# Hybrid stream step: the scan's decays behind the index heads, modulation blocks 4, 5 and 11 elsewhere

## The chip, the cores and the metric

The kernel runs on one core of a Trainium2 chip. The core has a matrix engine (TensorE, "PE" in the profile, its weight loads "PEld"), a vector engine (VectorE, "DVE"), a scalar engine (ScalarE, "ACT"), a general engine (GpSimd, "POOL") and a queue that starts transfers (SyncE, "SP"). They run side by side, and each works through its own list of instructions in the order written down. The metric is the device time of one execution in microseconds (us); lower is better.

## The reference, cut to what matters

One layer of a streaming encoder with d_model 1024 is computed for 512 new frames and 64 frames that follow a cache of 512; together 576 rows. A conditioning vector c gives six modulation vectors of 1024 numbers each:

```python
mod = (silu(c) @ w_ada + b_ada)            # 6 * 1024 columns
sh1, sc1, gt1, sh2, sc2, gt2 = split(mod, 6)
h = rms_normalize(x) * g_norm_mix * (1 + sc1) + sh1
q, k, v, qi, ki, wi, z, xbc, dt, gate = split(h @ w_in)
```

Branch A is sparse attention. Small index heads, `qi` (8 heads of 64) and `ki`, are turned by a rotation (rope) and give each query a score for every key; the 128 or 144 best keys of each query are kept, and attention runs over these. Branch B is a state-space scan: `dt` gives step sizes, and from them decays, `acs = cumsum(softplus(dt + dt_bias) * -exp(a_log))` within chunks, weigh the scan. Both branches are projected, gated and summed; `x = x + gt1 * mixed`. A gated feed-forward net follows, on `rms_normalize(x) * g_norm_ffn * (1 + sc2) + sh2`, and its result is added after a product with `gt2`.

## The kernel before, in words

**Number format.** Weights arrive as float32 (`raw`, two buffers) and are split into a high part `wh` (a copy on ScalarE) and a low part `wl` (raw minus high, on VectorE), three buffers each. Each product is three matmuls: high by high, high by low, low by high. Activations are split likewise (`hTh`, `hTl`).

**Stages.** Start: load, normalise, compute sh1 and sc1, make h. Then the first products with `w_in`: a small one (`misc`: ki, wi, dt), two gate columns, the index heads `qi0` and `qi1` (function `tm`, 256 columns each), then k, v, the first two groups of q, and gate columns as filler work for TensorE. While TensorE does these, VectorE computes scores and takes the best keys by repeated maxima (the index stage, until about 235 us). Attention follows per key head, with more filler columns; then the scan (about 470 to 800 us), the branch projections (to about 930), the output projection, the feed-forward net, and at the end the down projection `w_down` in eight columns of 128 with the residual (`x2r`) and the transposes back.

**Modulation blocks.** `w_ada` is worked on in blocks of 512 columns, u = 0 to 11. Blocks for sh1 and sc1 are made in the start. Blocks 4 and 5 are gt1, 6 and 7 sh2, 8 and 9 sc2, 10 and 11 gt2. `ada_columns(u, pool)` (line 765) makes one: four transfers of 512 KB (`adr`, two buffers), 16 VectorE instructions that accumulate (`aacc`), eight small matmuls that pick the sums (with a reserve, below), a copy `ra`, a transpose and an addition into `modc`. Before, blocks 4 and 5 are called behind the index stage's code (line 1174, pool `adx`), 6 to 9 in the branch projections (line 1528, pool `adv`), 10 and 11 ahead of the down projection (line 1816).

**Decays.** Behind `misc` stand the decays (from `dcol` to `acs_d`): softplus on tiles `dtp` and `e1` to `e3` ("e" in the profile) as a chain of small VectorE instructions, `dA`, then 15 small matmuls with the triangles `tri` and `ones` into PSUM, and their read-out into `nacs`, `edec`, `wst`, `acsT`.

**Index heads.** `key_stack` (line 1087) doubles the keys on GpSimd (`kisd`), transposes them on TensorE and splits them into `kis`. `rope` (line 966) rotates `x` (tile `tok`): two VectorE products into `tmpb`, one GpSimd product in place, one VectorE addition. `q_stack` (line 1106) transposes the heads and splits them into `qis`. Scores start from `kis` and `qis`.

**What sets the order.** The program isn't issued as written. `Plan` (from line 246) collects all instructions with their data dependences, gives each a cost (`cost`) and lays them out with a list scheduler (`order`, line 391): it takes the engine that is free first and gives it, of its ready instructions, the one of lowest rank; the rank is the place in the program minus an offset (`with R.prio(4000)` moves work ahead; weight splits after the first have it). An engine with something ready is never left idle on purpose. `R.slack` is a reserve: a TensorE instruction counts as ready only so many us after its inputs (0.25 by default, 3.0 for the pick matmuls). `with R.after(ops)` makes instructions count as ready only behind `ops`, in the plan alone. The order found is then fixed for each engine; on the chip an instruction waits for its true inputs. Buffers of a tag are handed out in program order: `px` has two PSUM slots and `py` two, so an instruction that gets a slot waits for all readers of the tile that had it before. A pool opens only when the pools closed ahead of it in the program are done (`R.close`): attention's pool behind `ix` and `adx`, the feed-forward net's behind `adv`.

Of the kernel before, what the change touches and what calls it, by code (L numbers as in the profile page):

```python
# [13 lines left out]
P = 128  # L14
# [225 lines left out]


NADA = 0
NADX = 2
NRAW, NWH = 2, 3
SLACK = 0.25

# [294 lines left out]
def build(tc, I, O):  # L541
# [13 lines left out]
    def px(name, tag="px"):  # L555
        return psum.tile([P, 512], F32, name=name, tag=tag, bufs=2)
# [409 lines left out]
    def rope(name, x, tab, h, rms):  # L966

        x4 = x.rearrange("p t (h d) -> p t h d", h=h)
        b = ap_.tile([P, 5, h, HD], F32, name=name + "rb", tag="tmpb", bufs=1)
        if rms:  # L970
            act.activation(b, x4, AF.Square)
            r = ap_.tile([P, 5, h], F32, name=name + "rr", tag="rr", bufs=2)
            vec.tensor_reduce(r, b, axis=AX.X, op=OP.add)
            rf = r.rearrange("p t h -> p (t h)")
            rstd_of(rf, rf, 5 * h, P, HD)
            vec.tensor_tensor(x4, x4, r[:, :, :, None].to_broadcast([P, 5, h, HD]), OP.mult)
        vec.tensor_tensor(b[..., 0:32], x4[..., 32:64], tab[:, :, None, 64:96].to_broadcast([P, 5, h, 32]), OP.mult)
# [56 lines left out]
    sync.dma_start(O["ki_sample"][0, 0], ki[:NS, 4, :])  # L1034


    dcol = cp.tile([P, 16], F32, name="dcol")
    for r in range(2):
        pool.tensor_copy(dcol[64 * r:64 * r + 64], dsk[64 * r:64 * r + 64].rearrange("p (b r) -> p r b", r=2)[:, r])
    act.activation(alg, alg, AF.Exp)  # L1040
    dtp = cp.tile([P, 5, 32], F32, name="dtp")
    e1 = ix.tile([P, 5, 32], F32, name="e1")
    e2 = ix.tile([P, 5, 32], F32, name="e2")
    e3 = ix.tile([P, 5, 32], F32, name="e3")
    vec.tensor_tensor(dtp, misc[:, :, 72:104], dtb[:, None, :].to_broadcast([P, 5, 32]), OP.add)
    act.activation(e1, dtp, AF.Abs)
    act.activation(e1, e1, AF.Exp, scale=-1.0)
    vec.tensor_scalar(e2, e1, 2.0, None, op0=OP.add)
    vec.reciprocal(e2, e2)
    vec.tensor_tensor(e1, e1, e2, OP.mult)  # L1050
    vec.tensor_tensor(e2, e1, e1, OP.mult)
    vec.tensor_scalar(e3, e2, 1.0 / 17.0, None, op0=OP.mult)
    for c in (15.0, 13.0, 11.0, 9.0, 7.0, 5.0, 3.0):
        vec.scalar_tensor_tensor(e3, e3, 1.0 / c, e2, op0=OP.add, op1=OP.mult)
    vec.scalar_tensor_tensor(e3, e3, 1.0, e1, op0=OP.add, op1=OP.mult)
    vec.tensor_scalar(dtp, dtp, 0.0, None, op0=OP.max)
    vec.scalar_tensor_tensor(dtp, e3, 2.0, dtp, op0=OP.mult, op1=OP.add)
    dA = e1
    vec.scalar_tensor_tensor(dA, dtp, -1.0, alg[:, None, :].to_broadcast([P, 5, 32]), op0=OP.mult, op1=OP.mult)
    pool.memset(dA[NS:P, 4, :], 0.0)  # L1060
    nacs = cp.tile([P, 5, 32], F32, name="nacs")
    wst = cp.tile([P, 5, 32], F32, name="wst")
    edec = cp.tile([P, 5, 32], F32, name="edec")
    p = px("pacs")
    p2 = px("ptot", "py")
    for c in range(5):
        pe.matmul(p[:, 32 * c:32 * c + 32], tri, dA[:, c, :], start=True, stop=True)
        pe.matmul(p2[:, 32 * c:32 * c + 32], ones, dA[:, c, :], start=True, stop=True)
    fl = lambda z: z.rearrange("p c h -> p (c h)")
    vec.tensor_scalar(fl(nacs), p[:, :160], -1.0, None, op0=OP.mult)  # L1070
    act.activation(fl(edec), p2[:, :160], AF.Exp)
    vec.tensor_tensor(fl(wst), p2[:, :160], fl(nacs), OP.add)
    act.activation(wst, wst, AF.Exp)
    vec.tensor_tensor(wst, wst, dtp, OP.mult)
    p = [px("pacsTa"), px("pacsTb", "py")]
    for c in range(5):
        o, i0 = (p[0][:32, P * c:P * c + P], P) if c < 4 else (p[1][:32, :NS], NS)
        pe.matmul(o, dA[:i0, c, :], tri[:i0, :i0], start=True, stop=True)
    acsT = ix.tile([32, T], F32, name="acsT")
    act.activation(acsT[:, :NP_], p[0][:32, :], AF.Copy)  # L1080
    act.activation(acsT[:, NP_:], p[1][:32, :NS], AF.Copy)
    acs_d = R.dram([32, T], F32, name="acs_d")
    sync.dma_start(acs_d, acsT)
# [22 lines left out]
    def q_stack(st, name, x, pair, h0, n_h):  # L1106


        p = px(f"{name}p")
        p2 = px(f"{name}q", "py")  # L1110
        for tb in range(4):
            pe.transpose(p[:, tb * P:(tb + 1) * P], x[:, tb, P * pair:P * pair + P], ident)
        pe.transpose(p2[:, 0:P], x[:, 4, P * pair:P * pair + P], ident)
        for i in range(2):
            for src, c0, n in ((p, (h0 + i) * NP_, NP_), (p2, n_h * NP_ + (h0 + i) * NS, NS)):
                d = st[:, c0:c0 + n]
                act.activation(d[0:64], src[64 * i:64 * i + 64, :n], AF.Copy)
                vec.tensor_tensor(d[64:128], src[64 * i:64 * i + 64, :n], d[0:64].bitcast(F32), OP.subtract)

    kis = key_stack(ix, "kis", "kis", ki, I["cache_ki"][0, 0].rearrange("(t p) d -> p t d", p=P))  # L1120
    qis = ix.tile([P, 8 * T], F32R, name="qis")
    for hf in range(2):
        x = ap_.tile([P, 5, 256], F32, name=f"qi{hf}", tag="tok", bufs=2)
        tm(f"qi{hf}", getw(), 256, x)
        rope(f"qi{hf}", x, cs2, 4, False)
        for pr in range(2):
            q_stack(qis, f"qis{hf}{pr}", x, pr, 4 * hf + 2 * pr, 8)


    masks = []  # L1130
# [5 lines left out]
    for b in (4, 1, 2, 3):  # L1136
        smp = b == 4
        n = T if smp else P * (b + 1)
        rows = NS if smp else P
        k0 = NP_ if smp else 0  # L1140
        s = ix.tile([P, n], F32, name=f"score{b}")
        for h in range(NIH // 2 if smp else NIH):
            q0 = 8 * NP_ + h * P if smp else h * NP_ + b * P
            q = qis[:, q0:q0 + P]
            w1 = wi2[:, h:h + 1] if smp else wi[:, b, h:h + 1]
            for c0, cn in (((0, TH), (TH, TH)) if smp else ((0, n),)):
                ps = px(f"pix{b}_{h}_{c0}", "py")
# [19 lines left out]
        vec.tensor_scalar(masks[b][:rows], s[:rows, :n], -2.0e38, NEG, op0=OP.is_gt, op1=OP.mult)  # L1167
# [714 lines left out]
```

## Time and profile before

| | us |
|---|---|
| median of 3 runs | 1392.15 |
| lowest and highest run | 1389.15, 1392.44 |
| the profiled execution | 1395.28 |
| its span, first to last instruction | 1393.5 |
| PE busy in the span | 1363.9 |

The profile comes from one execution. Helper calls issue all instructions, so every row has line 533, and rows are told apart by their tiles: `out<-in`, buffer numbers left out (`wh3` is `wh`, `e1` is `e`, `hTh` stays). A timeline row has start, duration, engine, instruction, tiles, shape, count; in brackets stands how long the engine was idle before it and what ended that. Neighbouring instructions of one kind are merged into a row with their count. A table by stage has for each stretch the busy time of each engine with its instruction count, the granted clock of PE as a share, the share of the DMA engines that was busy, and GB/s; for one tile it counts that tile's instructions alone. A float32 matmul that isn't split has two entries in the trace.

### The profile page before, as it was taken

The numbers are of one execution on the slowest core, as the hardware profiler recorded it, in microseconds if no ns is written. First come the engines' busy times: TensorE is split into PE (matmuls) and PEld (weight loads), VectorE is DVE, ScalarE is ACT, GpSimd is POOL, SyncE is SP. The second block draws the span as 40 slices with busy tenths as digits, with TensorE's granted clock in tenths as the row PEclk, the third lists the DMA queues.
The fourth block names the chain that finished last, engine by engine and source line by source line (L and its number), as shares of the span: only waits on it lengthen the run. The fifth ranks groups of instructions, "written<-read, shape, count | busy, mean of one in ns | idle before, by whom it ended". The sixth has DMA issues, their size and how long they took to land.

```text
span 1393.5 us, 27697 instructions
## 1 busy us (share of the span) xinstructions
PE 1363.9 (98%) x10801; PEld 1323.5 (95%) x10801; DVE 1052.8 (76%) x2099; ACT 721.8 (52%) x1496; POOL 243.2 (17%) x366
## 2 busy tenths in 40 slices
PE   7989999999999999999999999999999999999998
PEld 5989999999999999999999999999999999999998
DVE  4488999687877798989887688834899888875221
ACT  5435233667876667666665342225666666661221
POOL 1210001530310254655554200000000000000000
PEclk9999999999999999999999999999999999999999
DMA  9943345764754454544435598646233333346331
GB/s 283 281 140 92 87 119 151 171 153 122 166 134 126 136 143 123 145 125 143 130 110 172 177 311 262 206 136 189 72 92 102 96 91 92 90 130 202 107 109 29
DMA packets 268836, 200.17 MB, mean 144 GB/s; under 512 B 24993, under 2 KB 240193, under 8 KB 268705
## 3 DMA queue, kind: packets, MB, share of 16 engines
q1 hardware_dynamic: 265680, 187.39, 45.8%
q0 software_dynamic: 3024, 11.01, 4.3%
q8 instruction: 85, 1.39, 0.4%
q14 instruction: 47, 0.38, 0.1%
HBM read 157.81 MB, written 29.55 MB: 134 GB/s over the span
## 4 chain that ended last, share of the span: by engine, by line
PE 81%; DVE 7%; DMA 4%; issue 3%; ACT 2%; POOL 1%; SPq 1%; ACTq 0%; POOLq 0%; DVEq 0%
PE mm L533 59%; PE py L533 14%; PE px L533 9%; DVE score L533 1%; DMA raw<-in_w_in 1%; DVE aacc L533 1%; DVE wl L533 1%; DVE m L533 1%; SPq L533 1%; DMA stage<-y_d 1%; DMA adr<-in_w_ada 1%; DMA xt<-in_x_sample 1%; DMA wl<-raw 1%; ACT wh L533 0%; DMA bc<-acs_d 0%
## 5 line engine op out<-in xcount | busy, mean ns | idle before, releaser
L533 ACT ACTIVATE wh<-raw 128x1024 fp32r<-128x1024 f32 (+2 forms) x159 | 156.3, 985 | 245.4 <-PE mm L533 178.1
L533 PE MATMUL mm<-hTh,wl 128*128 128x288 f32 (+1 forms) x1024 | 235.8, 303 | 0.0
L533 PE MATMUL mm<-hTh,wh 128*128 128x288 f32 (+1 forms) x1024 | 235.0, 305 | 0.4 <-ACT hTh L533 0.4
L533 PE MATMUL mm<-hTl,wh 128*128 128x288 f32 (+1 forms) x1024 | 232.8, 303 | 0.0
L533 DVE TENSOR_TENSOR wl<-raw,wh 128x1024 fp32r<-128x1024 f32 (+2 forms) x116 | 139.9, 1208 | 84.4 <-ACT wh L533 81.4
L533 PEld LDWEIGHTS mm<-hTh,wh 128*128 128x128 f32 (+1 forms) x1024 | 167.4, 189 | 3.7 <-issue 1.3
L533 PEld LDWEIGHTS mm<-hTh,wl 128*128 128x128 f32 (+1 forms) x1024 | 167.8, 189 | 2.7 <-issue 1.4
L533 PEld LDWEIGHTS mm<-hTl,wh 128*128 128x128 f32 (+1 forms) x1024 | 166.8, 189 | 2.7 <-issue 1.4
L533 DVE SCALAR_TENSOR_TENSOR cu<-xc,wc,cu 128x579 f32<-128x579 f32 x96 | 84.7, 883 | 2.6 <-ACT cu L533 2.0
L533 PE MATMUL mm<-fh,wl 128*128 128x288 f32 x352 | 80.2, 299 | 0.9 <-DVE x2r L533 0.9
L533 PE MATMUL mm<-fh,wh 128*128 128x288 f32 x352 | 80.4, 298 | 0.1
L533 PE MATMUL mm<-fl,wh 128*128 128x288 f32 x352 | 80.5, 298 | 0.0
L533 PE MATMUL mm<-wl,hTh 128*128 128x256 f32 x256 | 73.6, 288 | 5.0 <-DVE wl L533 4.5
L533 PE MATMUL mm<-wh,hTl 128*128 128x256 f32 x256 | 73.0, 287 | 0.0
L533 PE MATMUL mm<-wh,hTh 128*128 128x256 f32 x256 | 72.6, 287 | 0.0
L533 DVE SCALAR_TENSOR_TENSOR aacc<-adr,sil,aacc 128x512 f32<-128x512 f32 x98 | 69.4, 746 | 0.9 <-DMA adr<-in_w_ada 0.7
L533 PEld LDWEIGHTS mm<-fh,wl 128*128 128x128 f32 x352 | 58.0, 189 | 1.9 <-DVE x2r L533 1.4
L533 PEld LDWEIGHTS mm<-fh,wh 128*128 128x128 f32 x352 | 58.1, 189 | 0.6 <-ACT wh L533 0.3
L533 PEld LDWEIGHTS mm<-fl,wh 128*128 128x128 f32 x352 | 58.1, 189 | 0.3 <-issue 0.2
L533 PE MATMUL mm<-yl,wh 128*128 128x288 f32 x256 | 54.9, 297 | 1.1 <-DVE yl L533 1.0
L533 PE MATMUL mm<-yh,wl 128*128 128x288 f32 x256 | 55.9, 297 | 0.0
L533 PE MATMUL mm<-yh,wh 128*128 128x288 f32 x256 | 55.1, 298 | 0.1
(439 smaller groups left out, 3768.4 us busy)
## 6 DMA issues: line engine op xcount, KB each, us to landing
raw<-in_w_in SPq DMA_DIRECT2D x80, 512.0 KB, 4.1
adr<-in_w_ada SPq DMA_DIRECT2D x48, 512.0 KB, 6.2
rawu<-in_w_gate_up SPq DMA_DIRECT2D x22, 512.0 KB, 3.9
raw<-in_w_gate_up SPq DMA_DIRECT2D x22, 512.0 KB, 3.8
wl<-raw POOLq DMA_DIRECT2D x21, 512.0 KB, 4.9
bc<-acs_d SPq DMA_DIRECT2D x32, 256.0 KB, 3.6
raw<-in_w_branch_ssm SPq DMA_DIRECT2D x16, 512.0 KB, 4.1
raw<-in_w_down SPq DMA_DIRECT2D x16, 512.0 KB, 3.6
```

Source lines behind the costliest of these rows:

```text
L533: getattr(engines[x.eng], x.fn)(*[real(a) for a in x.args], **{k: real(v) for k, v in x.kw.items()})
```

## The change

`NADX` goes from 2 to 1. The text of `key_stack`, `q_stack` and the loop over the two index heads moves as it is from behind the decays to ahead of them; `rope` now returns its last instruction, and the loop keeps it. The decays' 15 matmuls get a reserve of 3 us. The block loop behind the index takes block 4 alone and ties it to the first head's rotation; block 5 falls to the loop of `adv`, which now runs over 5 to 9 (its code is the same and depends on `NADX`). Block 11 moves from ahead of the loop over the eight columns of the down projection to ahead of the second of them. A list `masked` is filled and not used.

```diff
-NADX = 2
+NADX = 1
...
-        vec.tensor_tensor(x4, x4, b, OP.add)
+        return vec.tensor_tensor(x4, x4, b, OP.add)
...
+    kis = key_stack(ix, "kis", "kis", ki, I["cache_ki"][0, 0].rearrange("(t p) d -> p t d", p=P))
+    qis = ix.tile([P, 8 * T], F32R, name="qis")
+    ropes, masked = [], []
+    for hf in range(2):
+        x = ap_.tile([P, 5, 256], F32, name=f"qi{hf}", tag="tok", bufs=2)
+        tm(f"qi{hf}", getw(), 256, x)
+        ropes.append(rope(f"qi{hf}", x, cs2, 4, False))
+        for pr in range(2):
+            q_stack(qis, f"qis{hf}{pr}", x, pr, 4 * hf + 2 * pr, 8)
     dcol = cp.tile([P, 16], F32, name="dcol")
...
+    R.slack = 3.0
     p = px("pacs")
     p2 = px("ptot", "py")
...
         pe.matmul(o, dA[:i0, c, :], tri[:i0, :i0], start=True, stop=True)
+    R.slack = SLACK
     acsT = ix.tile([32, T], F32, name="acsT")
...
-    for hf in range(2):
-        x = ap_.tile([P, 5, 256], F32, name=f"qi{hf}", tag="tok", bufs=2)
-        tm(f"qi{hf}", getw(), 256, x)
-        rope(f"qi{hf}", x, cs2, 4, False)
-        for pr in range(2):
-            q_stack(qis, f"qis{hf}{pr}", x, pr, 4 * hf + 2 * pr, 8)
...
-    with R.prio(0):
-        for u in range(4, 4 + NADX):
+    for u, op in ((4, ropes[0]),):
+        with R.after([op]):
             ada_columns(u, adx)
...
-    ada_columns(11, adg, 1, 4)
-    vec.tensor_scalar(gt2h[:, 4:8], gt2[:, 4:8], 0.5, None, op0=OP.mult)
     yop = R.mkpool("yout", reuse_waits="tile")
     fd = (lambda k: fh[k], lambda k: fl_[k])
     for a in range(8):
+        if a == 1:
+            ada_columns(11, adg, 1, 4)
+            vec.tensor_scalar(gt2h[:, 4:8], gt2[:, 4:8], 0.5, None, op0=OP.mult)
         w = getw()
```

More of the change, by code (lines that the diff above doesn't have):

```diff
@@ L1034, in build @@
     sync.dma_start(O["ki_sample"][0, 0], ki[:NS, 4, :])
[L1037 to L1083, printed above, removed]
     def key_stack(pl, tag, name, new, cache, kd=None):
@@ L1124, in build @@
         tm(f"qi{hf}", getw(), 256, x)
-        rope(f"qi{hf}", x, cs2, 4, False)
+        ropes.append(rope(f"qi{hf}", x, cs2, 4, False))
         for pr in range(2):
             q_stack(qis, f"qis{hf}{pr}", x, pr, 4 * hf + 2 * pr, 8)
+    dcol = cp.tile([P, 16], F32, name="dcol")
+    for r in range(2):
+        pool.tensor_copy(dcol[64 * r:64 * r + 64], dsk[64 * r:64 * r + 64].rearrange("p (b r) -> p r b", r=2)[:, r])
+    act.activation(alg, alg, AF.Exp)
+    dtp = cp.tile([P, 5, 32], F32, name="dtp")
@@ new lines, in build @@
+    e1 = ix.tile([P, 5, 32], F32, name="e1")
+    e2 = ix.tile([P, 5, 32], F32, name="e2")
+    e3 = ix.tile([P, 5, 32], F32, name="e3")
+    vec.tensor_tensor(dtp, misc[:, :, 72:104], dtb[:, None, :].to_broadcast([P, 5, 32]), OP.add)
+    act.activation(e1, dtp, AF.Abs)
+    act.activation(e1, e1, AF.Exp, scale=-1.0)
+    vec.tensor_scalar(e2, e1, 2.0, None, op0=OP.add)
+    vec.reciprocal(e2, e2)
+    vec.tensor_tensor(e1, e1, e2, OP.mult)
+    vec.tensor_tensor(e2, e1, e1, OP.mult)
+    vec.tensor_scalar(e3, e2, 1.0 / 17.0, None, op0=OP.mult)
@@ new lines, in build @@
+    for c in (15.0, 13.0, 11.0, 9.0, 7.0, 5.0, 3.0):
+        vec.scalar_tensor_tensor(e3, e3, 1.0 / c, e2, op0=OP.add, op1=OP.mult)
+    vec.scalar_tensor_tensor(e3, e3, 1.0, e1, op0=OP.add, op1=OP.mult)
+    vec.tensor_scalar(dtp, dtp, 0.0, None, op0=OP.max)
+    vec.scalar_tensor_tensor(dtp, e3, 2.0, dtp, op0=OP.mult, op1=OP.add)
+    dA = e1
+    vec.scalar_tensor_tensor(dA, dtp, -1.0, alg[:, None, :].to_broadcast([P, 5, 32]), op0=OP.mult, op1=OP.mult)
+    pool.memset(dA[NS:P, 4, :], 0.0)
@@ new lines, in build @@
+    nacs = cp.tile([P, 5, 32], F32, name="nacs")
+    wst = cp.tile([P, 5, 32], F32, name="wst")
+    edec = cp.tile([P, 5, 32], F32, name="edec")
+    R.slack = 3.0
+    p = px("pacs")
+    p2 = px("ptot", "py")
+    for c in range(5):
+        pe.matmul(p[:, 32 * c:32 * c + 32], tri, dA[:, c, :], start=True, stop=True)
+        pe.matmul(p2[:, 32 * c:32 * c + 32], ones, dA[:, c, :], start=True, stop=True)
+    fl = lambda z: z.rearrange("p c h -> p (c h)")
+    vec.tensor_scalar(fl(nacs), p[:, :160], -1.0, None, op0=OP.mult)
@@ new lines, in build @@
+    act.activation(fl(edec), p2[:, :160], AF.Exp)
+    vec.tensor_tensor(fl(wst), p2[:, :160], fl(nacs), OP.add)
+    act.activation(wst, wst, AF.Exp)
+    vec.tensor_tensor(wst, wst, dtp, OP.mult)
+    p = [px("pacsTa"), px("pacsTb", "py")]
+    for c in range(5):
+        o, i0 = (p[0][:32, P * c:P * c + P], P) if c < 4 else (p[1][:32, :NS], NS)
+        pe.matmul(o, dA[:i0, c, :], tri[:i0, :i0], start=True, stop=True)
+    R.slack = SLACK
+    acsT = ix.tile([32, T], F32, name="acsT")
+    act.activation(acsT[:, :NP_], p[0][:32, :], AF.Copy)
@@ L1130, in build @@
+    act.activation(acsT[:, NP_:], p[1][:32, :NS], AF.Copy)
+    acs_d = R.dram([32, T], F32, name="acs_d")
+    sync.dma_start(acs_d, acsT)
     masks = []
@@ L1166, in build @@
             vec.match_replace(s[:rows, :n], m8[:rows], s[:rows, :n], -3.0e38)
-        vec.tensor_scalar(masks[b][:rows], s[:rows, :n], -2.0e38, NEG, op0=OP.is_gt, op1=OP.mult)
+        masked.append(vec.tensor_scalar(masks[b][:rows], s[:rows, :n], -2.0e38, NEG, op0=OP.is_gt, op1=OP.mult))
         if smp:
```

## The prediction

> **What bounds the kernel now.** I read the page first, then the table by stage, then the PE gaps one by one, then the queue of the engine that ended each gap.
>
> ```profile
> PE 1363.9 (98%) x10801; PEld 1323.5 (95%) x10801; DVE 1052.8 (76%) x2099; ACT 721.8 (52%) x1496; POOL 243.2 (17%) x366
> ```
>
> TensorE is busy for 1363.9 of 1393.5 us. The change removes no PE instruction, so it can only win back idle PE time, 29.6 us in all, and time in which PE ran slowly. The table by stage says where the edited region loses (columns: stretch, us, busy of PE, PEld, DVE, ACT, POOL with counts, granted clock, DMA share, GB/s).
>
> ```profile
> 60.00:80.00 20.00, 15.85 (x126) 15.66 (x125) 13.60 (x27) 5.11 (x8) 5.07 (x8) 0.90 0.82 248
> 80.00:100.00 20.00, 20.00 (x162) 19.67 (x162) 14.96 (x28) 7.58 (x18) 3.93 (x2) 0.93 0.40 114
> 260.00:280.00 20.00, 17.92 (x147) 17.48 (x146) 14.55 (x31) 13.77 (x28) 11.02 (x6) 1.00 0.56 124
> ```
>
> From 60 to 80 us PE is idle for 4.15 us, and the granted clock is 0.90 and 0.93 there instead of 1.00. PE's timeline shows one gap and a slow stretch behind it:
>
> ```profile
> 73.14 0.28 PE L533 MATMUL mm<-wh,hTh 128*128 128x256 f32 x1
> 73.26 0.27 PE L533 MATMUL mm<-wl,hTh 128*128 128x256 f32 x1
> 77.68 0.58 PE L533 MATMUL mm<-wl,hTh 128*128 128x256 f32 x1 [4.15 <-DVE wl L533]
> ...
> 78.91 0.42 PE L533 MATMUL mm<-wh,hTh 128*128 128x256 f32 x1
> 79.12 0.42 PE L533 MATMUL mm<-wl,hTh 128*128 128x256 f32 x1
> ...
> 82.54 0.35 PE L533 MATMUL mm<-wl,hTh 128*128 128x256 f32 x1
> ```
>
> PE ran dry at 73.53 in the second product of the index heads (qi1) and waited until 77.68 for the low half `wl` of a weight split. Before the gap a matmul started every 0.12 us, behind it every 0.21 us, until 82.54. Next, VectorE's queue ahead of that `wl`, the same engine's share for block 4 alone (tile aacc), and ScalarE's part:
>
> ```profile
> 68.46 0.48 DVE L533 TENSOR_SCALAR aacc<-adr,sil 128x512 f32<-128x512 f32 x1 [0.58 <-DMA adr<-in_w_ada]
> ...
> 74.79 0.74 DVE L533 SCALAR_TENSOR_TENSOR aacc<-adr,sil,aacc 128x512 f32<-128x512 f32 x1
> 75.46 1.03 DVE L533 SCALAR_TENSOR_TENSOR e<-e,e 128x160 f32<-128x160 f32 x3
> 76.41 1.22 DVE L533 TENSOR_TENSOR wl<-raw,wh 128x1024 fp32r<-128x1024 f32 x1
> ```
> ```profile
> 68.00:76.40 8.40, 0.00 (x0) 0.00 (x0) 5.33 (x8) 0.97 0.71 195
> ```
> ```profile
> 70.38 2.03 ACT L533 ACTIVATE wh<-raw 128x1024 fp32r<-128x1024 f32 x2 [0.23 <-PE mm L533]
> ```
>
> `wh`, which `wl` needs, was done at 70.38 + 2.03/2 = 71.40. `wl` began at 76.41 only because eight instructions of modulation block 4 and the decay chain (tile e) stood ahead of it. VectorE works in the order written down, so the stall is one of order.
>
> **The change, part by part.** *Block 4 behind the first rotation.* Its eight instructions leave this queue. An instruction starts about 0.07 us before its predecessor's end (74.79 + 0.74 = 75.53, the next at 75.46), so they hold 5.33 - 8 x 0.07 = 4.77 us. `wl` would start at 76.41 - 4.77 = 71.64, be done at 72.86, and PE needs it at 73.53: the 4.15 us go, with 0.67 us to spare. What may be put in this place instead is the rest of the decay chain, and the key stack of the index, which could not run so early before:
>
> ```profile
> 76.40:95.00 18.60, 3.53 (x30) 3.25 (x30) 1.66 (x6) 0.00 (x0) 0.12 (x1) 0.83 0.42 117
> ```
> ```profile
> 94.42 1.29 DVE L533 TENSOR_TENSOR kis<-px,kis 128x512 fp32r<-128x512 f32 x2 [0.25 <-ACT kis L533]
> ```
>
> These are 1.66 us (six instructions of the chain) and 1.29 us. With both ahead, `wl` is done at 72.86 + 2.95 = 75.81 and 2.28 us of stall stay. Gain between 1.87 and 4.15; I take 4.15, because the computed case stands on the queue as it is.
>
> *The clock.* 77.68 to 82.54 is 4.86 us at a pitch of 0.213, some 23 matmuls. At 0.12 they take 2.74, so 2.1 us are lost to the low clock. A gap of 4.15 us was followed by it. The stretch 260 to 280, which has 2.08 us idle, kept 1.00. So without the gap the 2.1 us come back, and with 2.28 us left it is open. I take 2.1, with 0 as the other end. The Trainium skill, "TensorE: Matmul & The Clock Gate", section "Why this matters for your kernels", warns of PE gaps over about 3 us; by that rule a rest of 2.28 us would keep the full clock too, and both rows here agree with it.
>
> *Index heads ahead of the decays.* The two PSUM slots of tag px are given out in program order. Before, the index's transposes took theirs behind the decays' sums:
>
> ```profile
> 67.07 0.72 POOL L533 COPY kisd<-misc 128x640 f32<-128x640 f32 x1 [2.72 <-issue]
> 85.14 1.49 DVE L533 TENSOR_TENSOR tok<-tok,tmpb 128x1280 f32<-128x1280 f32 x1 [2.85 <-POOL tok L533]
> ```
> ```profile
> 91.23 1.06 PE L533 MATMUL px<-tri,e 128*32 128x128 f32 x8
> ...
> 92.79 0.60 PE L533 MATMUL px<-ident,kisd 128*128 128x128 f32 x4
> ...
> 96.14 0.60 PE L533 MATMUL px<-ident,tok 128*128 128x128 f32 x4
> ```
>
> The keys were ready at 67.79 and turned at 92.79; the first heads were rotated at 86.63 and turned at 96.14. In the new order they need no decay. That moves some 10 to 20 us of latency, which PE filled with matmuls, so it is worth nothing by itself. It does make the order tighter: the first heads' transposes now stand right behind their rotation, as the second heads' did, and those waited. All waits of PE from 85 to 300 us:
>
> ```profile
> PE px L533 <- DVE P L533: 1.6, 1, 1.6
> PE px L533 <- DVE tok L533: 0.7, 1, 0.7
> PE py L533 <- ACT lg L533: 0.6, 1, 0.6
> PE mm L533 <- DMA wl<-raw: 0.5, 1, 0.5
> PE mm L533 <- DVE wl L533: 0.3, 1, 0.3
> PE py L533 <- DVE qis L533: 0.3, 1, 0.3
> ```
>
> I charge one more wait of the tok kind: 0.7 us lost. Its ends are 0 and 0.7 + 0.9, since the two rotations on POOL differed by 0.87 us:
>
> ```profile
> 81.30 3.81 POOL L533 TENSOR_TENSOR tok<-tok,cs 128x1280 f32<-128x1280 f32 x1 [13.51 <-DVE tmpb L533]
> 104.37 2.94 POOL L533 TENSOR_TENSOR tok<-tok,cs 128x1280 f32<-128x1280 f32 x1 [17.26 <-DVE tmpb L533]
> ```
>
> The Trainium skill, "SBUF — State Buffer", section "Who interferes with whom", says that a VectorE instruction with two SBUF inputs contends with a GpSimd instruction that reads SBUF. By it, decays and splits beside both rotations would make both take 3.81 and the sum would be 0.9 us less; the longer rotation here did have VectorE instructions beside it.
>
> *The reserve of 3 us* moves the 15 small decay matmuls later in PE's order; they are the same in number. If VectorE were later still than the reserve, the weight matmuls queued behind them on PE would wait. No row of before has PE waiting there, so nothing is charged. The whole stretch is ordered anew, though. For that the six rows above are the nearest price, 4.0 us in all: as much may go or come. I take zero and keep both ends.
>
> *Block 5 to the branch stage.* It leaves the index stage and joins blocks 6 to 9 behind 811 us, with four loads of 512 KB on SP, 16 VectorE instructions, eight small matmuls (16 entries in the trace), a transpose and two small VectorE copies:
>
> ```profile
> 118.00:240.00 122.00, 0.85 (x16) 0.32 (x16) 11.31 (x16) 1.00 0.40 113
> ```
> ```profile
> 906.00:933.00 27.00, 27.00 (x205) 27.00 (x204) 10.30 (x16) 6.58 (x10) 0.96 (x8) 1.00 0.33 101
> ```
> ```profile
> 885.74 0.28 DVE L533 COPY ra<-px 128x128 f32<-128x128 f32 x1
> 904.91 0.28 DVE L533 COPY ra<-px 128x128 f32<-128x128 f32 x1
> ```
> ```profile
> 834.04 4.74 SPq L533 DMA_DIRECT2D adr<-in_w_ada  x2
> ...
> 933.62 2.00 SPq L533 DMA_DIRECT2D x<-x_d  x4
> ```
>
> Two blocks end 19.2 us apart, so a fifth ends at 904.9 + 19.2 = 924.1, ahead of the next stage's loads at 933.62. VectorE is free for 16.7 of the 27 us from 906 and needs 11.3. Cover is there; cost zero on both sides, as PE does the same work in either place. If SP's queue loses that cover, the price is in the slower rival.
>
> *Block 11 behind the first column of the last stage.* Before, its instructions stood ahead of the residual x2r, for which PE's transposes waited:
>
> ```profile
> 1267.51 4.72 DVE L533 SCALAR_TENSOR_TENSOR aacc<-adr,sil,aacc 128x512 f32<-128x512 f32 x7
> ...
> 1273.95 0.79 DVE L533 SCALAR_TENSOR_TENSOR x2r<-mm,gt2h,x2r 128x32 f32<-128x32 f32 x3
> ```
> ```profile
> 1274.25 0.28 PE L533 MATMUL px<-ident,x2r 128*32 128x128 f32 x1 [0.88 <-DVE x2r L533]
> ```
>
> Gain 0.9 us, with 0 as the other end. Its results are needed only from the fifth column on.
>
> **The sum:** 4.15 + 2.1 + 0.9 - 0.7 = 6.45 us. The profiled execution took 1395.28 us (span 1393.5 and 1.78 around it) and would take 1388.8. The median of the runs shown is 1392.15, 3.13 lower; against it 1385.7.
>
> **The rivals.** *VectorE's queue stays full* (22%): the chain and the key stack take block 4's place. For it: the planner never leaves an engine idle that has something ready, and the decays are ready early. Against it: the 0.67 us of room and the rank of `wl`. Gain 1.87 + 0 + 0.9 - 0.7 = 2.1 us, 1390.1. *The index stage gains as well* (14%): with 11.31 us less on VectorE the 4.0 us of waits go and none is added: 6.45 + 0.7 + 4.0 = 11.2, 1381.0. For it: the stage's splits and rotations share VectorE with that block. Against it: the largest of the waits, 1.6 us for P, lies in the attention, behind the index. *SP held by block 5's loads* (9%), the one that ends slower: a load of modulation weights waits on SP until VectorE has read the buffer, 4.74 us in the row at 834, and the weights queue behind it. A weight tile feeds 48 matmuls, 27/205 x 48 = 6.3 us; holds beyond that lead stop PE. Four loads held so long are 19.0 us, 12.7 beyond the lead: 12.7 - 6.45 = 6.2 us slower, 1398.4. Against it: PE is busy for all 27 us of the row from 906, right behind four such blocks. *The change doesn't do what it says* (5%): the planner places the decays where they were and only the last stage gains 0.9, 1391.3.
>
> **How the numbers follow.** The forecast has 50%, and its own range is 1383 to 1388. A measurement of this kernel can tell about 0.3% (4.2 us) from no change. Faster by more: 50 + 14 = 64%. Within it: 22 + 5 = 27%. Slower: 9%. The range goes from the second rival's 1381.0 less half the spread of the runs shown (1.6) to no change with 1.6 more: 1379.5 to 1394.0; outside lie the slower rival and little else.
>
> **What would show it.** Right: no PE gap in the qi1 product, granted clock 1.00 from 60 us on, transposes of kisd ahead of the matmuls with tri, no aacc instruction until the first rotation has ended, no PE wait for x2r at the start of the last stage. Wrong: a PE wait for `wl` of over 2 us between 60 and 100, waits for tok of over 1 us, SP holds ahead of the branch weights with PE idle behind 811, or x loads later than PE's need.

## The result, and the profile after

The changed kernel took 1384.67 us (median of 6 runs, 1383.1 to 1386.53), the kernel before 1390.7 us beside it (median of 6, 1389.15 to 1392.44). The ratio is 0.9956, 95% interval 0.9943 to 0.9969: 6.1 us faster. The profiled execution took 1384.84 us (span 1383.1). That of before took 1395.28, which is 4.6 above the median of its runs here, so the 10.4 us between the two profiles overstate the gain.

The page of the changed kernel, its line of engines:

```profile
PE 1357.8 (98%) x10801; PEld 1319.1 (95%) x10801; DVE 1053.1 (76%) x2099; ACT 721.3 (52%) x1496; POOL 246.4 (18%) x366
```

Same counts, and PE is busy for 6.1 us less: it ran less of its work slowly. Idle PE time fell from 29.6 to 25.3 us. Where, in the table by stage (60 to 80 and 80 to 100 answer to the two rows of before):

```profile
60.00:80.00 20.00, 18.99 (x160) 18.81 (x161) 13.20 (x27) 6.41 (x11) 4.14 (x7) 1.00 0.53 163
80.00:100.00 20.00, 19.44 (x165) 19.23 (x164) 12.92 (x20) 6.84 (x14) 5.95 (x2) 1.00 0.45 139
```

From 60 to 80 PE did 160 matmuls instead of 126, at a granted clock of 1.00 instead of 0.90 and 0.93. The gap in the qi1 product and the slow stretch behind it are gone. But PE's waits from 60 to 120 (us in total, times, longest) are not:

```profile
PE px L533 <- DMA kisd<-in_cache_ki: 2.3, 1, 2.3
PE py L533 <- DVE wst L533: 1.0, 1, 1.0
PE px L533 <- DVE kis L533: 0.9, 1, 0.9
PE mm L533 <- DVE wl L533: 0.6, 1, 0.6
```

They are 4.7 us where before had 5.1 (4.1 for `wl`, 0.7 and 0.3). PE's timeline of the changed kernel shows the first and the third in their places, and VectorE's what became of `wl`:

```profile
60.09 0.63 PE L533 MATMUL px<-ident,kisd 128*128 128x128 f32 x4 [2.26 <-DMA kisd<-in_cache_ki]
...
70.12 0.33 PE L533 MATMUL px<-ident,kisd 128*128 128x128 f32 x1 [0.92 <-DVE kis L533]
...
75.62 0.40 PE L533 MATMUL mm<-wh,hTh 128*128 128x256 f32 x2
```
```profile
72.50 0.33 DVE L533 SCALAR_TENSOR_TENSOR e<-dtp,alg 128x160 f32<-128x160 f32 x1
74.42 2.36 DVE L533 TENSOR_TENSOR wl<-raw,wh 128x1024 fp32r<-128x1024 f32 x2 [1.60 <-ACT wh L533]
81.98 1.49 DVE L533 TENSOR_TENSOR tok<-tok,tmpb 128x1280 f32<-128x1280 f32 x1 [3.15 <-POOL tok L533]
89.02 0.88 DVE L533 TENSOR_SCALAR aacc<-adr,sil 128x512 f32<-128x512 f32 x2
```

The transposes of the cached keys now stand in PE's order ahead of the index heads' products, and their transfer had not landed: PE stood for 2.26 us, then 0.92 for the split of the first transposes. The decay chain ended at 72.83, ahead of `wl`, and `wl` began at 74.42, not at the forecast 71.64; it waited for `wh`, with nothing else to do. `wh` in turn had waited on ScalarE for PE:

```profile
73.33 2.01 ACT L533 ACTIVATE wh<-raw 128x1024 fp32r<-128x1024 f32 x2 [0.23 <-PE mm L533]
```

So PE, held 3.2 us by the keys, came later to the product (75.62), and the split of its weights came later with it. What the split costs when the keys don't hold PE is seen in a4 below. Block 4 (aacc) began at 89.02, behind the first rotation's end at 83.47.

The second place is the way from the index to the attention. From 130 to 300 us, before and then after:

```profile
130.00:300.00 170.00, 166.93 (x1282) 164.03 (x1281) 151.84 (x343) 75.21 (x129) 33.43 (x24) 1.00 0.53 137
```
```profile
130.00:300.00 170.00, 169.39 (x1279) 166.53 (x1278) 155.41 (x362) 81.37 (x147) 34.12 (x27) 1.00 0.51 133
```

PE was idle for 3.07 us there and now for 0.61. Two small waits are left up to 480 us (the lists of before are in the prediction):

```profile
PE py L533 <- ACT lg L533: 0.6, 1, 0.6
PE py L533 <- DVE qst L533: 0.2, 1, 0.2
```

The attention's scores (all 160 matmuls of `kst` by `qst`; the columns are lowest, median and longest duration, then first and last start) began 19 us earlier. Before and after:

```profile
L533 PE MATMUL py<-kst,qst x160: 220/297/440, 270.2 to 457.8; 128*128 128x128 f32 x32, 128*128 128x288 f32 x32, 128*128 128x256 f32 x32, 128*128 128x384 f32 x32
```
```profile
L533 PE MATMUL py<-kst,qst x160: 220/296/468, 251.1 to 447.2; 128*128 128x128 f32 x32, 128*128 128x288 f32 x32, 128*128 128x256 f32 x32, 128*128 128x384 f32 x32
```

In the last stage the waits of PE for the residual, from 1200 us on, are now these two; the third of before, 0.88 us at 1274.25, is gone:

```profile
PE mm L533 <- DVE x2r L533: 0.9, 2, 0.6
PE py L533 <- DVE x2r L533: 0.6, 1, 0.6
```

### The profile page after: what moved, and what is told of

It reads as the page before. It is cut to its first block, busy times and chain, and to the rows that moved or that the text cites. A ratio compares the mean times of both kernels' runs of the same rounds, so it can differ in the third digit from the quotient of the medians.

```text
span 1383.1 us, 27717 instructions
## 1 busy us (share of the span) xinstructions
PE 1357.8 (98%) x10801; PEld 1319.1 (95%) x10801; DVE 1053.1 (76%) x2099; ACT 721.3 (52%) x1496; POOL 246.4 (18%) x366
## 4 chain that ended last, share of the span: by engine, by line
PE 84%; DVE 7%; DMA 4%; ACT 2%; issue 1%; SPq 1%; POOL 0%; ACTq 0%; DVEq 0%; POOLq 0%
PE mm L533 62%; PE py L533 13%; PE px L533 8%; DVE score L533 1%; DMA stage<-y_d 1%; DVE wl L533 1%; DMA raw<-in_w_in 1%; DVE m L533 1%; SPq L533 1%; DMA xt<-in_x_sample 1%; DVE y L533 0%; DVE xlS L533 0%; DVE qis L533 0%; DMA kd<-in_cache_k 0%; DMA bc<-acs_d 0%
## 5 line engine op out<-in xcount | busy, mean ns | idle before, releaser
L533 PE MATMUL mm<-hTl,wh 128*128 128x288 f32 (+1 forms) x1024 | 230.0, 301 | 0.3 <-DVE hTl L533 0.3
```

The source lines that it names most:

```text
L533: getattr(engines[x.eng], x.fn)(*[real(a) for a in x.args], **{k: real(v) for k, v in x.kw.items()})
```

## The experiments

The theory was the prediction's: block 4's place in VectorE's queue is the stall, and the rest of the edits are worth little. Its rival, after the first look at the traces: the edits act together, through the order that the planner finds, and the gain is that no new wait came up further on. First each part was put into the kernel before by itself, then each but block 11 was taken out of the changed kernel; the reserve was not run alone. All ratios are to the kernel before, from runs on the same chip, with their 95% interval; the changed kernel's is 0.9956.

**Block 4 alone behind the first rotation** (e1; block 5 stays in the index stage, decays as before).

```diff
-    with R.prio(0):
-        for u in range(4, 4 + NADX):
-            ada_columns(u, adx)
+    with R.after([ropes[0]]):
+        ada_columns(4, adx)
+    ada_columns(5, adx)
```

> The kernel before with one part alone: block 4 tied behind the first rotation, all else as it was. Theory (block 4 ahead of the split was the stall): the 4.15 us gap in the second heads' product and the low clock behind it go; 4 to 6.3 us faster than before. First rival (VectorE's load in the index stage was the price): the work is only moved a little, so less than 1 us. Second rival (the order of heads and decays was the price): the chain still stands ahead of the split, 2 us of gap stay, and 2 to 4 us are won.

Measured: 1403.59 us against 1390.15, ratio 1.0097 (1.0081 to 1.0114), 13 us slower. The wait for `wl` is gone, and another is in its place. PE's timeline and the table by stage of this kernel:

```profile
69.75 0.28 PE L533 MATMUL mm<-wh,hsS 128*128 128x256 f32 x1
73.33 0.64 PE L533 MATMUL px<-e,tri 128*128 128x32 f32 x2 [3.31 <-DVE e L533]
```
```profile
70.00:76.00 6.00, 2.69 (x14) 2.67 (x13) 4.11 (x11) 0.88 (x1) 0.12 (x1) 0.70 0.07 11
76.00:82.00 6.00, 6.00 (x29) 5.17 (x29) 1.26 (x4) 1.93 (x5) 0.00 (x0) 0.50 0.28 89
```

With block 4 away the planner put the decays' matmuls early in PE's order; on the chip VectorE's chain for `e` was late, and PE stood for 3.31 us and then ran at half clock until 82.6. A second loss lies at the end of the attention. This kernel, then before:

```profile
460.00:480.00 20.00, 17.75 (x114) 15.38 (x113) 16.97 (x47) 13.37 (x31) 0.00 (x0) 1.00 0.20 54
```
```profile
460.00:480.00 20.00, 20.00 (x145) 19.10 (x144) 15.32 (x27) 10.91 (x22) 3.81 (x17) 1.00 0.48 138
```

114 matmuls in 20 us where before has 145. The attention's scores still began late, at 275.9, and its filler columns were used up early: the last one was read out at 451.65, and the attention ended at 485.4. The theory falls in this form: block 4's place alone is no gain. Without the reserve on the decays' matmuls the wait only moves; a5 below has the tie with the reserve.

**Block 5 alone to the branch stage** (e2).

```diff
-NADX = 2
+NADX = 1
```

> The kernel before with one part alone: block 5 made in the branch projections. Theory: the gap of 4.15 us at 73 stays, since block 5 isn't in that queue; within 1 us of before. First rival (VectorE's load): attention starts some 10 us earlier, the waits between 85 and 300 us shrink, and 3 to 5 us are won. Second rival: no change.

Measured: 1390.9, ratio 1.0006 (0.9994 to 1.0017). No difference, though the first score of the attention moved from 270.2 to 255.2 and PE's wait for `wl` was 3.3 us. An earlier start of the attention is worth nothing by itself.

**Index heads alone ahead of the decays** (e3; both blocks as before).

```diff
+    kis = key_stack(ix, "kis", "kis", ki, I["cache_ki"][0, 0].rearrange("(t p) d -> p t d", p=P))
...
+    for hf in range(2):
...
     dcol = cp.tile([P, 16], F32, name="dcol")
```

> The kernel before with one part alone: the index heads' code ahead of the decays, both blocks still behind the index and untied, no reserve. Theory: block 4 still fills the decay chain's pauses, so the split stays late and the gap is 3 to 5 us; the key stack's new place adds the wait of about 2 us for the cached keys seen in the changed kernel; from 1 us faster to 2 us slower. Second rival (the order is what counts): 4 us or more faster.

Measured: 1387.02, ratio 0.9978 (0.9969 to 0.9988), 3.1 us faster. Here too a wait for the keys takes the place of that for `wl`; PE's timeline of this kernel:

```profile
60.84 0.63 PE L533 MATMUL px<-ident,kisd 128*128 128x128 f32 x4 [2.06 <-DVE tmpb L533]
```

The row names VectorE's `tmpb`, which ended just then; what these four transposes read are the cached keys, as the new ones are copied into `kisd` only at 65.69. It is 2.06 us with the full clock behind it, where the 4.15 us had half a clock behind them. The gap of 3 to 5 us for the split, which was expected to stay, did not come, although block 4 stands ahead of `wl` as before and `wl` begins only 1 us earlier than the 76.41 of before:

```profile
75.36 1.21 DVE L533 TENSOR_TENSOR wl<-raw,wh 128x1024 fp32r<-128x1024 f32 x1
```

PE, with the keys ahead in its order, comes to it later. So the heads' place takes the stall away with block 4 where it was. The only part that pays by itself beyond its interval (block 11's, below, does not) is one that I had costed at nothing.

**Block 11 alone** (e4).

```diff
     for a in range(8):
+        if a == 1:
+            ada_columns(11, adg, 1, 4)
+            vec.tensor_scalar(gt2h[:, 4:8], gt2[:, 4:8], 0.5, None, op0=OP.mult)
```

> The kernel before with one part alone: block 11 behind the first column of the last stage. Theory: PE's wait of 0.88 us for the residual goes and some interleaving with it, 0.9 to 1.2 us faster. Rival (the wait is covered by the second column's matmuls anyway): under 0.3 us.

Measured: 1388.77, ratio 0.9991 (0.9981 to 1.0002): 1.4 us by the medians, with no change just inside the interval. The wait of 0.88 us for `x2r` is gone in its trace as in that of the changed kernel, so the mechanism is shown and its time is not told from nothing.

Next, the parts taken out of the changed kernel.

**Without the tie** (a1).

```diff
-    for u, op in ((4, ropes[0]),):
-        with R.after([op]):
-            ada_columns(u, adx)
+    ada_columns(4, adx)
```

> The changed kernel with one part undone: block 4 no longer tied behind the first rotation. My first theory (block 4's place is the stall) has lost its ground with the part alone; it would still ask for 4 us or more slower than the changed kernel. The new theory (the index heads' transposes standing ahead of the decays' matmuls in TensorE's order is what removes the stall, as the heads alone brought 3 us) expects no gap over 1 us for a split and 0 to 2 us slower than the changed kernel, that is 1384.5 to 1387.

Measured: 1392.54 against 1392.78, ratio 1.0001 (0.9993 to 1.001). The whole gain is gone, where 0 to 2 us were expected, yet the index stage is as quick as in the changed kernel. As in e3, block 4 stands ahead of `wl` again (`wl` begins at 75.48) and PE doesn't wait for it: beside the heads' new place the tie is not what keeps the stall away. The time is lost later, from 220 to 310 us among other places:

```profile
PE py L533 <- DVE qst L533: 2.5, 2, 1.6
```

**Block 5 kept in the index stage, behind block 4** (a2).

```diff
-NADX = 1
+NADX = 2
...
             ada_columns(u, adx)
+    ada_columns(5, adx)
```

> The changed kernel with one part undone: block 5 back behind the index, untied. New theory: block 5 decides when the index stage's pool closes and attention begins (270 us before, 251 in the changed kernel), and with it how many filler columns are left for attention; begun later, 1 to 3 us slower than the changed kernel. Rival (off the path, as the part alone showed no difference): within 1 us of it.

Measured: 1401.61, ratio 1.0065 (1.0049 to 1.008). The scores of the attention began at 274.0 instead of 251.1, and the attention's end shows the hole of e1:

```profile
460.00:480.00 20.00, 18.16 (x116) 15.74 (x114) 15.97 (x38) 12.45 (x26) 0.00 (x0) 1.00 0.20 54
480.00:500.00 20.00, 18.49 (x122) 17.88 (x123) 13.67 (x20) 13.68 (x34) 8.96 (x27) 0.91 0.55 164
```

So block 5's move, worth nothing in the old order, carries more than the whole gain in the new one.

**Without the reserve** (a3).

```diff
-    R.slack = 3.0
...
-    R.slack = SLACK
```

> The changed kernel with one part undone: no reserve on the decays' 15 matmuls. Theory (the reserve covers a decay chain that runs later than planned, as in the run with block 4 alone tied, where TensorE waited 3.3 us for it): a wait of 1 to 3 us for tile e returns, and the kernel is 1 to 3 us slower than the changed one. Rival: behind the heads the PSUM slots hold the decays' matmuls back anyway, so no wait for e and within 0.5 us.

Measured: 1397.01, ratio 1.0031 (1.0019 to 1.0043). No wait for `e` came back. PE waited in the start of the attention (220 to 310 us), and the attention's end has a hole:

```profile
PE mm L533 <- DMA wl<-raw: 2.2, 1, 2.2
PE px L533 <- DVE P L533: 1.6, 1, 1.6
```
```profile
460.00:480.00 20.00, 16.64 (x107) 13.96 (x106) 14.45 (x32) 12.11 (x26) 0.47 (x4) 1.00 0.29 84
```

What the reserve saves here is not the wait that it was made for: it changes the order of everything behind it.

**Decays' code ahead of the heads again, the rest of the change kept** (a5).

```diff
+    dcol = cp.tile([P, 16], F32, name="dcol")
...
     kis = key_stack(ix, "kis", "kis", ki, I["cache_ki"][0, 0].rearrange("(t p) d -> p t d", p=P))
...
-    dcol = cp.tile([P, 16], F32, name="dcol")
```

> The changed kernel with one part undone: decays' code ahead of the index heads again, with block 4 tied, block 5 moved, the reserve kept and block 11 as changed. Theory (the heads' place is what counts): slower than the changed kernel by 3 us or more, with TensorE waiting for a split or for tile e around 70 us. Rival (the reserve alone cures the wait for e that the tie brought): as fast as the changed kernel within 1 us, and no wait for cached keys at 58.

Measured: 1393.81, ratio 1.001 (1.0 to 1.0019). No keys to wait for at 58, no wait for the `wl` of qi1, and from 50 to 130 us it is 2.9 us quicker than the changed kernel, some 5 us quicker than before (table below). So with the reserve, and the heads where they were, block 4's new place does win the start nearly as forecast. All of that and some 7 us more is lost behind it; from 125 to 310 us this is its longest wait:

```profile
PE mm L533 <- DMA wl<-raw: 2.5, 1, 2.5
```

**A reserve of 3 us on the keys' transposes, too** (a4). If the new key wait is the price of the change, this is the way to have the gain without it.

```diff
+    R.slack = 3.0
     kis = key_stack(ix, "kis", "kis", ki, I["cache_ki"][0, 0].rearrange("(t p) d -> p t d", p=P))
+    R.slack = SLACK
```

> The changed kernel with a reserve of 3 us also on the nine transposes of the index's key stack. Theory (in the changed kernel TensorE's wait of 2.26 us for the cached keys at 58 has taken the place of the wait for the split): that wait goes. If nothing takes its place, 2 us faster than the changed kernel (about 0.994 of before); if the queue behind it then meets the late split again, the wait moves to 70 to 76 us and the time stays within 1 us of the changed kernel. Any order behind it may shift as well, for which the other runs showed up to 8 us in attention.

Measured: 1393.18 against 1391.84, ratio 1.0006 (0.9994 to 1.0018). The key wait is gone. Without it PE waits 0.61 us for the `wl` of qi1, with the decay chain and two of the three pieces of the keys' split ahead of it in VectorE's queue:

```profile
75.03 0.39 PE L533 MATMUL mm<-wl,hTh 128*128 128x256 f32 x1 [0.61 <-DVE wl L533]
```

From 50 to 130 us it is 2.5 us quicker, but 2.6 us are lost from 220 to 300 and 5.0 from 500 to 860, where PE's two longest waits are

```profile
PE px L533 <- ACT sto L533: 1.8, 2, 1.6
PE mm L533 <- ACT yh L533: 1.4, 3, 0.6
```

**Block 5 in the index pool, but called behind the first two heads of q** (b3): is it its rank that holds up the attention, or that the attention's pool opens only when block 5 is done?

```diff
-NADX = 1
+NADX = 2
...
+    ada_columns(5, adx)
```

> The kernel with block 5 kept behind the index, but with its rank behind the first two query groups' rotations instead of ahead of the key rotation; VectorE's load and the closing of the pool are as in that run. Theory (VectorE reaches the first query rotation late because block 5 ranks ahead of it, which is when attention begins): first attention matmul at 251 to 260 instead of 274, and 4 to 8 us faster than that run, about 1.000 of before. Rival (VectorE's total load in the index stage, or the pool that stays open, sets the start): attention still begins at 270 or later and the time stays at 1.005 to 1.008 of before.

Measured: 1397.43, ratio 1.0032 (1.0022 to 1.0043). The first score came at 277.1, no earlier than with the high rank, but for another reason. The first query rotation begins on VectorE at 257.80 in a2, and in b3 at 236.32, as early as in the changed kernel (235.64):

```profile
257.80 1.49 DVE L533 TENSOR_TENSOR tok<-tok,rr 128x1280 f32<-128x1280 f32 x1 [2.89 <-POOL rr L533]
```
```profile
236.32 1.49 DVE L533 TENSOR_TENSOR tok<-tok,rr 128x1280 f32<-128x1280 f32 x1 [2.81 <-POOL rr L533]
```

What is late in b3 is block 5 itself. Its pick matmuls stand in PE's order ahead of transposes for the attention's keys and queries, and PE waits for its sums until 267. PE's two longest waits in b3 from 220 to 310 us:

```profile
PE px L533 <- DVE aacc L533: 3.4, 2, 3.1
PE py L533 <- DVE ra L533: 1.5, 1, 1.5
```

So the rank does hold up the rotation, and the low rank trades that for a late block 5. The rest of the fourteen traces fit: where block 5 lies in the index stage at its high rank (before, e1, e3, e4, a2, f1), the first query rotation begins between 251 and 263 us and the scores between 265 and 276; where it doesn't lie there, between 233 and 244 and between 251 and 261. That VectorE has 11.3 us more to do in the index stage fits these numbers as well, and no run tells this from the rank. The opening of the pool by itself doesn't set the start: in the kernel before VectorE writes `vst`, a tile of the attention's pool, at 239.05, 31 us ahead of the first score. Whether it sets the order that holds b3 up is not shown.

**One filler column more for the attention's end** (f1 in a2, f2 in the changed kernel). One of the gate columns that PE did in the scan goes to the last key head of the attention. If the hole at 460 us is lack of filler, f1 closes it and f2 gains nothing.

```diff
-    LATE = 1
-    FILL = [5, 5, 5, 5]
+    LATE = 0
+    FILL = [5, 5, 5, 6]
```

> The kernel with block 5 kept behind the index, with the filler column that stood in the scan given to attention's last key head (none late, six there instead of five); the order is the same up to that column. Theory (fillers run out at 453 us, 28 us ahead of attention's end, and TensorE then lacks work: 116 matmuls in 20 us instead of 145 to 151): the column's 6.4 us of matmuls fall into that hole, 3 to 6 us faster than that run, about 1.001 to 1.004 of before. Rival (the tail's loss isn't lack of filler work): the same as that run within 1 us.

> The changed kernel with the same filler column given to attention's last key head. Theory: its fillers end 15 us ahead of attention's end and TensorE lacks no work there, so the column is only moved: within 1 us of the changed kernel (0.995 to 0.997 of before). Rival (every column moved ahead helps): 3 us faster.

Measured: f1 1404.22, ratio 1.0079 (1.0062 to 1.0095); f2 1386.28, ratio 0.9955 (0.9941 to 0.997). In f1 the hole is closed, in the row from 460; then the scan from 740 to 860 of f1, and the same stretch of the changed kernel:

```profile
460.00:480.00 20.00, 20.00 (x140) 18.77 (x140) 16.04 (x37) 11.93 (x24) 0.00 (x0) 1.00 0.24 68
...
740.00:860.00 120.00, 114.61 (x927) 108.52 (x924) 87.05 (x158) 47.90 (x93) 27.27 (x34) 0.99 0.66 213
```
```profile
740.00:860.00 120.00, 118.54 (x958) 113.84 (x957) 89.15 (x154) 42.03 (x70) 14.04 (x15) 1.00 0.78 247
```

PE does 140 matmuls instead of a2's 116. From 740 to 860 it does 31 fewer than the changed kernel (f1 is some 10 us behind by then, so that it isn't quite the same work), and it waits 3.1 us for `sto` alone. So the hole was lack of filler, as the theory had it, but the 3 to 6 us didn't come: what the column saved there was lost in the scan that it came from. f2 took the same column from the scan and lost nothing by it, so this too depends on the order.

**All kernels side by side.** The table is my own sum from the start times of the matmuls in each trace: each matmul is given the usual step to the next one of its form in the changed kernel, the steps are added up, and at the same sum the kernel's time is compared with the changed kernel's. The entries are us lost against the changed kernel in each of five stretches of its time. The start, 860 to 1240 us and the end are left out, so that rows don't add up to the whole. Single profiles scatter: kernels that share their start and their last stage differ there by up to 3 us. The profiles of before and of e4 lie 4.6 and 3.9 us above the medians of their kernels, so their rows are too high in sum.

| kernel | ratio | 50-130 | 130-300 | 300-460 | 460-500 | 500-860 |
|---|---|---|---|---|---|---|
| before | 1 | 2.4 | 3.9 | 1.1 | -0.2 | 2.1 |
| e1, block 4 alone | 1.0097 | 3.5 | 5.3 | 2.5 | 8.3 | 1.1 |
| e2, block 5 alone | 1.0006 | 0.8 | 2.1 | 0.7 | 0.5 | 0.4 |
| e3, heads alone | 0.9978 | 0.3 | 1.4 | 0.6 | -0.2 | 1.4 |
| e4, block 11 alone | 0.9991 | 2.5 | 3.1 | 1.1 | -0.2 | 0.3 |
| a1, no tie | 1.0001 | -1.0 | 3.3 | 0.1 | 0.6 | 2.2 |
| a2, block 5 kept | 1.0065 | 0.2 | 8.0 | 0.8 | 7.2 | 1.1 |
| a3, no reserve | 1.0031 | -0.8 | 4.7 | -0.8 | 5.7 | 0.1 |
| a5, decays first | 1.001 | -2.9 | 6.2 | -0.3 | 0.6 | 3.8 |
| a4, keys' reserve | 1.0006 | -2.5 | 2.7 | 1.2 | 0.8 | 5.0 |
| b3, block 5 low | 1.0032 | 0.4 | 10.1 | 0.5 | 1.1 | -0.4 |
| f1, block 5 kept, filler | 1.0079 | 0.1 | 8.9 | 0.8 | 0.2 | 10.7 |
| f2, change with filler | 0.9955 | 0.7 | 0.0 | 0.1 | -0.5 | -0.3 |

The column 130-300 tells the changed order apart: all that lacks one of its parts loses 1.4 to 10 us there, four of them with a quicker index stage. The parts are not additive: the four that ran alone multiply to 1.0097 x 1.0006 x 0.9978 x 0.9991 = 1.0072, slower by 10 us, and with the reserve they are 6 us faster. If the reserve is counted at what its removal cost (0.9956 / 1.0031), the product is 0.9997, still some 6 us short. No kernel here beats the changed one; f2 equals it.

## Why the prediction was right, and where it was not

The total came out as forecast: 6.45 us off the median, 6.1 measured, and 1384.67 lies in the range and in the likeliest case's own. Two terms behind it were wrong, in opposite directions.

- **Gap and clock, 4.15 + 2.1.** Both are gone, and the granted clock is 1.00 from 60 us on. What failed is the step "the computed case stands on the queue as it is": the decay chain and the keys' split did go ahead of `wl`, as the first rival had it, and the room of 0.67 us was not there. They cost less than that rival's 2.28 us: 0.61 in a4, where the keys don't hold PE, and nothing in a5. a5 shows that block 4's move, with the reserve beside it, is enough to remove the stall. That it is what removed it in the changed kernel is not shown, as e3 and a1 have no such gap with block 4 in its old place. The row from 260 to 280, from which the prediction took that 2.08 us of idle time keep the clock, has them in pieces of at most 1.56, and says nothing of one gap of that length.
- **One more wait, 0.7.** It did not come: no wait for tok is left, and the old one (0.7) and that for `qis` (0.3) went. In its place came a kind that I had not thought of, the key stack ahead in PE's order: 2.26 and 0.92 us, then 0.6 for another `wl` and 1.0 for `wst`, whose PSUM slot the scores now take over. I had written that the keys' earlier turn "is worth nothing by itself", and looked at when the copied keys were ready, not at when the cached ones landed. The sum of the stretch: 4.15 + 2.1 + 0.7 + 0.3 - 2.26 - 0.92 - 0.6 - 1.0 = 2.5 us, as the table's 2.4; forecast 5.55.
- **Order from 85 to 300 us, taken as zero with 4.0 either way.** From 130 to 300 it brought 3.9 us, 2.5 of them idle time of PE in the rows above, and 1.1 more up to 460; against e4, whose order is that of before up to the last stage, it is 3.1 and 1.1. The value chosen failed, the end "4.0 us in all: as much may go" held. The second rival was right in this place and wrong in the other: the waits for P went, though they lie behind the index. Its mechanism is in the traces: with block 5 out of the queue VectorE begins the key rotation at 122 us instead of 241 and the first query rotation at 236 instead of 256. In e2 the same shift brought no time. The taking out of single parts shows that this gain hangs on the tie, block 5's move, the heads' place and the reserve at once.
- **The reserve, nothing charged.** Right in that no weight matmul waited behind the decays; wrong in that it is worth nothing: without it the changed kernel loses 0.75%, by order and not by a wait for the chain (1.0031 against 0.9956).
- **Block 5, zero.** Its cost in the branch stage is zero, as argued: the last of five blocks there was read out at 914.96 us, and the next stage's loads started at 923.60.

```profile
914.96 0.28 DVE L533 COPY ra<-px 128x128 f32<-128x128 f32 x1
```
```profile
923.60 1.96 SPq L533 DMA_DIRECT2D x<-x_d  x4
```

  Alone it gained nothing either (e2). Its worth beside the other parts, 1.0065 without it against 0.9956, was not in the forecast. The slower rival, SP held by the loads, did not come about: PE's waits from 800 to 940 us are 0.9 for `yh` and 0.6 for `yl`, none for a weight.
- **Block 11, 0.9.** The wait went. The sum of the table, taken over the end of the kernel from 1240 us on, has 1.2 us for before; every kernel with block 11 in its old place loses 0.8 to 1.7 us there, every one with it moved 0.0 to 0.2. The kernel with this alone gains 1.4 by its medians, with zero inside the interval. Right in mechanism, and in size as far as can be told.

So 5.55 became 2.5 and 0 became something between 2.4 and 5. The higher figure is the table's, from a profile of before that lies 4.6 us above the median; the lower is what the measured 6.1 us leave after 2.5 for the start and 1.2 for block 11. The forecast hit its total in part by luck: had the order further on come out as in a1 or a4, with the same gap filled, the time would have been that of before. What stays open is why just this set of orders leaves the start of the attention without a wait: no single placement was found that does it.

## What to carry to other kernels

In a kernel whose order a list scheduler finds and the queues then keep, an edit that takes away one stall also moves everything behind it: judge a set of edits together, run the parts both alone and left out, and look at the stages behind the one that was edited. Before you count a stall as won, ask what stands next in the waiting engine's order, and whether the input of each of those, transfers too, is there by then. A low rank doesn't make a piece of work harmless if another queue has to wait for it (b3). Filler work is a budget: what TensorE spends before and in a stage can be missing at its end, and a column moved there can be missing where it came from (f1), or not (f2).

## What the runs showed of the hardware

How long a PE gap must be to cost clock is not one number here. In a2 PE stood for 2.10 us, and its timeline slows down 1.2 us after the gap:

```profile
61.67 0.63 PE L533 MATMUL px<-ident,kisd 128*128 128x128 f32 x4 [2.10 <-DMA kisd<-in_cache_ki]
...
62.73 0.28 PE L533 MATMUL mm<-wl,hTh 128*128 128x256 f32 x1
...
63.00 0.41 PE L533 MATMUL mm<-wh,hTh 128*128 128x256 f32 x1
63.21 0.41 PE L533 MATMUL mm<-wl,hTh 128*128 128x256 f32 x1
```

The step goes from 0.12 to 0.21 us. In the changed kernel the same wait, 2.26 us, was followed by a granted clock of 1.00 from 60 to 80, and in b3 so was one of 2.4 us. In f2 the wait was 2.8 us, and the table by stage has the clock at 0.72 behind it:

```profile
60.00:65.00 5.00, 2.25 (x11) 2.29 (x12) 0.43 (x2) 0.80 (x1) 4.56 (x7) 0.72 0.91 293
```

The prediction's sentence on the Trainium skill ("TensorE: Matmul & The Clock Gate", section "Why this matters for your kernels", gaps over about 3 us) is borne out by the changed kernel and by b3; f2 lies at its edge, and a2 speaks against it. All seven gaps of over 3 us in the fourteen traces behind the first 10 us (3.11 to 4.15 us long) were followed by a lower clock. So a gap of 2 to 3 us may or may not cost clock, and an estimate should hold both. A slow stretch also came with no gap to explain it: in e3 the clock was 0.75 from 105 to 110 us, with PE busy throughout and no wait of over 0.3 us from 93 to 120.

```profile
105.00:110.00 5.00, 5.00 (x35) 4.10 (x34) 4.47 (x9) 2.75 (x8) 0.00 (x0) 0.75 0.39 124
```

The second rotation's product on GpSimd took 4.00 us in the changed kernel and the first 2.94; before, the first was the long one (3.81) and the second the short. GpSimd and VectorE of the changed kernel:

```profile
79.01 2.94 POOL L533 TENSOR_TENSOR tok<-tok,cs 128x1280 f32<-128x1280 f32 x1 [5.95 <-DVE tmpb L533]
94.78 4.00 POOL L533 TENSOR_TENSOR tok<-tok,cs 128x1280 f32<-128x1280 f32 x1 [12.84 <-DVE tmpb L533]
```
```profile
94.56 1.40 DVE L533 SCALAR_TENSOR_TENSOR aacc<-adr,sil,aacc 128x512 f32<-128x512 f32 x2
98.82 1.49 DVE L533 TENSOR_TENSOR tok<-tok,tmpb 128x1280 f32<-128x1280 f32 x1 [2.85 <-POOL tok L533]
```

Beside the first VectorE was idle (3.15 us, in the row at 81.98 above). Beside the second it worked on block 4 until 95.96, 1.18 us into the product, and the product took 1.06 us longer: GpSimd all but stood while VectorE worked there.
